# Last MoE of a two-layer trunk: expert rows added to x in SBUF by one-hot matmuls instead of scatter-adds to DRAM

## The chip, the cores and the metric

The kernel runs on 1 core of one Trainium2 chip. The metric is the device time of one execution in microseconds (us), the median of the runs shown. The profile and the trace come from one further execution on the same core; line numbers (L1236) are those of the kernel before.

## What is computed

A trunk of two layers. Each layer has a mixer and then an expert-choice mixture of experts (MoE): every expert takes the 64 latent tokens (of 512) with the highest routing weight, and its output rows are added to x. In the first layer a stream of 256 context tokens goes through the same experts; the second, last layer has the 512 latent tokens only, and its x is the output.

```python
def _expert_choice_ffn(h, router_w, w_gate, w_up, w_down):
    b, n_tok, _ = h.shape
    cap = EC_CAPACITY * n_tok // N_EXPERTS            # 2 * 512 // 16 = 64
    probs = jax.nn.softmax((h @ router_w).astype(jnp.float32), axis=-1)
    aff, idx = lax.top_k(jnp.swapaxes(probs, 1, 2), cap)
    xs = h[bidx, idx]
    hid = jax.nn.silu(einsum('becd,edf->becf', xs, w_gate)) * einsum('becd,edf->becf', xs, w_up)
    out = jnp.einsum('becf,efd->becd', hid, w_down) * aff[..., None]
    return jnp.zeros_like(h).at[bidx, idx].add(out.astype(h.dtype))
...
xl = xl + g2_l * _expert_choice_ffn(_modulate(_rms(xl, norm2_g[i]), sh2_l, sc2_l), ...)
```

All is float32. D_MODEL and MOE_FF are 1024, there are 16 experts, and the weights of one expert are three matrices of 1024x1024, 12.6 MB.

## The kernel before

The work of the last layer's MoE runs in two functions. `outer` (L1123) finishes the mixer's output projection, so that x stands in SBUF as the tile `xl` (128 x 4 x 1024, in pool `big`); routes it (`route_`, which leaves in `st` the token numbers `g` for gathers, the routing weights `af`, and the row numbers `sc`); writes the normalized rows to DRAM (`xh_l`, L1076); starts the gather of the first two experts' rows (`moe_gather`, L1189); and writes x itself to the output in DRAM (`base_write`, L1184), on which the experts then add. `experts` (L1246) loops over the 16 experts e = 0 to 15:

- `load_experts` issues the six loads of an expert on SP's queue: two halves each of `wg`, `wu`, `wd`, 2 MB a load, in the order of use. The buffers are taken in a ring written out by hand, `WT1 = "mmbbbbnnnb"`: ten buffers from three pools, so load n waits for TensorE (PE) to be done with load n - 10. The last letter is the fifth buffer of `big`, the one in which x stood.
- `gate_up` (L1236): for each half j (gate, up), 8 blocks k and 2 halves h a matmul of the 64 gathered rows against 512 columns; in the trace such a float32 matmul is two MATMUL rows, 64 rows for an expert. Then silu on ScalarE (ACT, L1239) and the product on VectorE (DVE, L1240) give `hid`.
- `turn_hid` (L1305, L1306): four transposes of `hid` on PE into `hT`, copied back by ACT.
- `down` (L1321, L1324): 32 MATMUL rows against `wd` into `oe`; partitions 0 to 63 hold the first 512 columns of the 64 rows, 64 to 127 the second 512. DVE scales by the routing weight and the gate into `ob`, and GpSimd (POOL, L1325) issues an indirect DMA that adds the 128 half rows of `ob` to rows `sc` of the output in DRAM (a scatter-add).
- After an odd e the rows of the next two experts are gathered (L1189) and transposed (`moe_turn`, L1198, L1203, L1205).

The tiles `hT` and `oe` share four PSUM buffers of the pool `b`; `gu` and `gT` share two of the pool `d`. In the last layer the order of the instructions on an engine is set by the framework's scheduler, and each engine carries it out in that order.

## Time and profile before

| | |
|---|---|
| median of 3 runs | 2016.27 us (2015.25 to 2017.24) |
| the profiled execution | 2015.42 us |
| its span, first to last instruction | 2013.7 us |
| PE busy in the span | 1824.0 us (91%) |
| DVE, ACT, POOL busy | 823.0, 586.4, 119.2 us |
| bytes moved by DMA | 545.62 MB, 271 GB/s over the span |

The span is 1.72 us shorter than the time of the same execution. The stages follow one another: the first layer's mixer to about 480 us, its experts to about 1090, the second mixer to about 1530, and the last layer's experts from there to the end. A profile row of the timeline gives start, length, engine, line, operation, output<-input, count, and in brackets how long the engine had been idle before and what released it.

### The profile page before, as it was taken

The page shows a single profiled execution, that of the slowest core. Times are in us where ns is not written, and L with a number is a line of the kernel's source. Part 1 is how long each engine was busy: PE and PEld are TensorE (multiplying, and loading weights), DVE is VectorE, ACT ScalarE, POOL GpSimd, SP SyncE. Part 2 cuts the span into 40 slices and gives each one's busy share as a digit, 9 for nine tenths or more (in the row PEclk, how much of TensorE's full clock was granted, in tenths as well). Part 3 has the DMA queues.
Part 4 walks back from the last instruction along what each step waited for, and adds up shares of the span by engine and source line. Part 5 has one row for each costly group of instructions (what it writes and reads, how often), then busy time and mean ns, then how long its engine had stood idle before and what let it go on. Part 6 is the DMA issues. An engine that isn't in the chain of part 4 may idle for free.

```text
span 2013.7 us, 28802 instructions
## 1 busy us (share of the span) xinstructions
PE 1824.0 (91%) x11900; PEld 1058.1 (53%) x11900; DVE 823.0 (41%) x2016; ACT 586.4 (29%) x1240; POOL 119.2 (6%) x118
## 2 busy tenths in 40 slices
PE   6999999999799999999996989999985997878776
PEld 5788888677433333333333778986762422222222
DVE  5797876676610101011104597976752100000000
ACT  5656465424210101011103565554330000000000
POOL 0000000000010111011000000000000000000000
PEclk9999999999699999999997989999987999999999
DMA  8352433246499999999985543211448999999997
GB/s 311 131 188 83 160 113 112 83 161 254 165 373 403 404 402 404 411 403 402 397 348 191 176 149 104 73 33 58 177 192 355 417 417 417 423 417 416 424 418 275
DMA packets 76403, 545.62 MB, mean 271 GB/s; under 512 B 8720, under 2 KB 15008, under 8 KB 51952
## 3 DMA queue, kind: packets, MB, share of 16 engines
q1 hardware_dynamic: 61312, 501.26, 62.6%
q0 software_dynamic: 14960, 42.53, 7.1%
q8 instruction: 93, 1.52, 0.3%
q14 instruction: 38, 0.31, 0.0%
HBM read 522.25 MB, written 21.50 MB: 270 GB/s over the span
## 4 chain that ended last, share of the span: by engine, by line
PE 36%; issue 29%; DMA 21%; DVE 7%; ACT 3%; POOL 3%; POOLq 0%; SPq 0%; ACTq 0%; DVEq 0%
DMA w<-wu 6%; DMA w<-wg 6%; DMA w<-wd 4%; PE gu L1236 4%; PE pt L416 3%; PE pt L418 2%; PE pt L417 2%; PE ao L839 2%; PE pf L416 2%; PE pf L417 2%; PE pf L418 2%; DMA xh_l<-xo 2%; PE ro L727 2%; PE macc L276 2%; PE oe L1321 1%
## 5 line engine op out<-in xcount | busy, mean ns | idle before, releaser
L1236 PE MATMUL gu<-w,xsT 128*64 128x512 f32 x2048 | 476.4, 617 | 50.6 <-DMA w<-wu 32.8
L1236 PEld LDWEIGHTS gu<-w,xsT 128*64 128x64 f32 x2048 | 153.4, 142 | 350.9 <-issue 271.0
L1321 PE MATMUL oe<-w,hid 128*64 128x512 f32 x1024 | 234.6, 610 | 9.7 <-ACT hid L1306 9.6
L1240 DVE TENSOR_TENSOR hid<-hid,gu 128x512 f32<-128x512 f32 x32 | 22.0, 687 | 462.9 <-ACT hid L1239 462.9
L1239 ACT ACTIVATE hid<-gu 128x512 f32<-128x512 f32 x32 | 19.1, 597 | 526.0 <-PE gu L1236 526.0
L1321 PEld LDWEIGHTS oe<-w,hid 128*64 128x64 f32 x1024 | 74.3, 140 | 157.1 <-issue 138.6
L417 PE MATMUL pt<-ws,hh 128*128 128x256 f32 x448 | 127.9, 285 | 5.0 <-DVE ws L411 5.0
L416 PE MATMUL pt<-ws,hh 128*128 128x256 f32 x448 | 130.8, 292 | 0.0
L418 PE MATMUL pt<-ws,hl 128*128 128x256 f32 x448 | 128.1, 286 | 0.0
L1324 DVE SCALAR_TENSOR_TENSOR ob<-oe,afl,g 128x512 f32<-128x512 f32 x32 | 24.0, 751 | 221.4 <-PE oe L1321 221.4
L1293 PE MATMUL guc<-w,xsT 128*32 128x512 f32 x1024 | 113.2, 594 | 0.0
L410 ACT ACTIVATE ws<-wraw 128x256 fp32r<-128x256 f32 x192 | 72.8, 411 | 83.6 <-PE pt L418 31.9
L416 PEld LDWEIGHTS pt<-ws,hh 128*128 128x128 f32 x448 | 85.8, 191 | 9.1 <-issue 8.6
L411 DVE TENSOR_TENSOR ws<-wraw,ws 128x256 fp32r<-128x256 f32 x192 | 76.7, 419 | 33.6 <-ACT ws L410 33.2
L417 PEld LDWEIGHTS pt<-ws,hh 128*128 128x128 f32 x448 | 85.7, 191 | 5.7 <-DVE ws L411 5.5
L418 PEld LDWEIGHTS pt<-ws,hl 128*128 128x128 f32 x448 | 85.8, 191 | 0.1
L1205 ACT ACTIVATE xsT<-gT,ab 128x128 f32<-128x128 f32 x80 | 36.6, 458 | 144.2 <-PE gT L1198 116.8
L416 PE MATMUL op<-ws,mh 128*128 128x256 f32 x256 | 74.9, 293 | 3.1 <-ACT mh L908 3.1
L817 ACT ACTIVATE p<-sc,mx 128x768 f32<-128x768 f32 (+1 forms) x80 | 65.2, 816 | 33.9 <-DVE mx L815 30.5
L417 PE MATMUL op<-ws,mh 128*128 128x256 f32 x256 | 74.0, 290 | 0.0
L418 PE MATMUL op<-ws,ml 128*128 128x256 f32 x256 | 73.5, 289 | 0.3 <-DVE ml L909 0.3
L815 DVE TENSOR_REDUCE mx<-sc 128x1 f32<-128x768 f32 (+1 forms) x80 | 66.4, 847 | 10.8 <-PE sc L811 10.2
(385 smaller groups left out, 3187.1 us busy)
## 6 DMA issues: line engine op xcount, KB each, us to landing
w<-wg SPq DMA_DIRECT2D x63, 2048.0 KB, 26.4
w<-wd SPq DMA_DIRECT2D x63, 2048.0 KB, 22.9
w<-wu SPq DMA_DIRECT2D x62, 2048.0 KB, 16.1
mw<-mod_w SPq DMA_DIRECT2D x80, 512.0 KB, 4.3
wraw<-w_in SPq DMA_DIRECT2D x48, 512.0 KB, 3.6
wo<-wo SPq DMA_DIRECT2D x24, 384.0 KB, 3.5
mw<-mod_a SPq DMA_DIRECT2D x16, 512.0 KB, 10.7
xh_l<-xo POOLq DMA_DIRECT2D x8, 512.0 KB, 12.4
```

The source lines that it names most:

```text
L276: nc.tensor.matmul(acc[32 * q:32 * q + 32, :256], self.scT[:, k, :], wt[:, q * 256:(q + 1) * 256], start=k == k0, stop=k == k0 + 1)
L410: nc.scalar.activation(t[:, 0], src, AF.Copy)
L411: nc.vector.tensor_tensor(t[:, 1], src, t[:, 0].bitcast(F32), op=ALU.subtract)
L416: nc.tensor.matmul(out, lh, rh, start=first, stop=False)
L417: nc.tensor.matmul(out, lh, rl, start=False, stop=False)
L418: nc.tensor.matmul(out, ll, rh, start=False, stop=last)
L727: nc.tensor.matmul(ol[64 * h:64 * h + 64, :], v, ws[h][:, :L], start=t == 0, stop=t == 5)
L815: nc.vector.tensor_reduce(mx, s[:, :n], axis=AX.X, op=ALU.max, negate=True)
L817: nc.scalar.activation(ptl[m][:, :n], s[:, :n], AF.Exp, bias=mx, accum_out=sm[:, m, t:t + 1])
L1236: self.pe(nc.tensor.matmul(d[64 * h:64 * h + 64, j, :], xl[:, k, x0:x0 + CAPL], W(j, k)[:, h * 512:(h + 1) * 512], start=k == 0, stop=k == ...
L1293: self.pe(nc.tensor.matmul(dc[32 * q:32 * q + 32, :], xc[:, k, c0:c0 + CAPC], W(q // 2, k)[:, (q % 2) * 512:(q % 2) * 512 + 512], start=k ...
L1321: self.pe(nc.tensor.matmul(o[64 * h:64 * h + 64, :], hid[:, 1, c * P + hh * 64:c * P + hh * 64 + 64], W(2, k)[:, h * 512:(h + 1) * 512], s ...
```

## The change

The routine `base_write` is no longer called in the last layer, and `xl` stays in its buffer: the ring of weight buffers has nine places. After `down` the rows `ob` go to a new function `combine`. It makes two one-hot matrices of 128x512 (DVE compares the numbers 0, 2, 4, ... with the row numbers, for each half h), splits `ob` into a rounded part `hi` (ACT) and the rest `lo` (DVE), both in the format float32r, and, for each of the 4 token tiles and both halves, lets PE multiply the one-hot columns with `hi` and `lo` into a PSUM tile `cb`, which DVE adds to x in SBUF. After the last expert each token tile is written to the output on SP's queue. The first layer is unchanged.

```diff
-WT1 = "mmbbbbnnnb"
+WT1 = "mmbbbbnnn"
...
+        if i == DEPTH - 1:
+            r["sf"] = self.cst([NE], nm="sf")
+            nc.vector.tensor_copy(r["sf"], sc)
...
-            self.base_write(x, base, not ctx or s)
+            if ctx:
+                self.base_write(x, base, s)
...
+        if not ctx:
+            self.iota = self.t("iota", [L], "iota")
+            nc.sync.dma_start(self.iota, self.a["iota2"])
...
-            self.down(e, W, hid, st[0], bl)
+            ob = self.down(e, W, hid, st[0])
+            if ctx:
+                self.scatter(bl, ob, st[0], e)
+            elif e < NE - 2:
+                late = lambda e=e, ob=ob: self.combine(e, ob, st[0])
+            else:
+                late = None
+                self.combine(e, ob, st[0], base_l if e == NE - 1 else None)
...
+    def combine(self, e, ob, st, dst=None):
+        nc = self.nc
+        oh = []
+        for h in range(2):
+            t = self.t("oh", [L], "oh", F32R)
+            nc.vector.tensor_scalar(t, self.iota, st["sf"][:, e:e + 1], -float(h), op0=ALU.subtract, op1=ALU.is_equal)
+            oh.append(t)
+        hi = self.t("obs", [L], "obh", F32R)
+        lo = self.t("obs", [L], "obl", F32R)
+        nc.scalar.activation(hi, ob, AF.Copy)
+        nc.vector.tensor_tensor(lo, ob, hi.bitcast(F32), op=ALU.subtract)
+        for t in range(4):
+            for h in range(2):
+                p = self.b("cb")
+                nc.tensor.matmul(p, oh[h][:, t * P:(t + 1) * P], hi, start=True, stop=False)
+                nc.tensor.matmul(p, oh[h][:, t * P:(t + 1) * P], lo, start=False, stop=True)
+                xx = self.xt[0][:, t, h * 512:(h + 1) * 512]
+                nc.vector.tensor_tensor(xx, xx, p, op=ALU.add)
+            if dst is not None:
+                nc.sync.dma_start(dst[t * P:(t + 1) * P], self.xt[0][:, t])
...
-            k.open(cw, ob=(2 if not last else 6, 0), g2=(2 if not last else 1, 0))
+            k.open(cw, ob=(2, 0), g2=(2 if not last else 1, 0))
...
+                k.open(cw, iota=(1, 0), oh=(2, 0), obs=(2, 0))
```

The tile `cb` comes from the same four PSUM buffers as `hT` and `oe`.

Line numbers in listings of the changed program are those of the changed kernel. What the change does to the order on PE, between the `down` of one expert and that of the next, in the middle of the last layer. Before (`oe` is the product with wd, `gu` the gate and up products, one matmul of the listing being two MATMUL rows of the trace, `hT` the transposes):

```order
L1305 MATMUL hT_14119<-ident_66,hid_14114 128x128 x4
L1321 MATMUL oe_14143<-w_14077,hid_14114 64x512 x8
L1321 MATMUL oe_14143<-w_14079,hid_14114 64x512 x8
L1236 MATMUL gu_14175<-w_14163,xsT_14134 64x512 x8
L1236 MATMUL gu_14175<-w_14165,xsT_14134 64x512 x8
```

Now, at the same place (`obh`, `obl` are `hi` and `lo`):

```order
L1361 MATMUL oe_14257<-w_14153,hid_14188 64x512 x8
L1348 MATMUL cb_14332<-obh_14328,oh_14324 128x512
L1348 MATMUL cb_14336<-obh_14328,oh_14326 128x512
L1348 MATMUL cb_14340<-obh_14328,oh_14324 128x512
L1348 MATMUL cb_14344<-obh_14328,oh_14326 128x512
L1349 MATMUL cb_14332<-obl_14329,oh_14324 128x512
L1349 MATMUL cb_14336<-obl_14329,oh_14326 128x512
L1241 MATMUL gu_14288<-w_14276,xsT_14248 64x512 x8
L1349 MATMUL cb_14340<-obl_14329,oh_14324 128x512
L1349 MATMUL cb_14344<-obl_14329,oh_14326 128x512
L1348 MATMUL cb_14348<-obh_14328,oh_14324 128x512
```

The first product with `obh` stands directly behind the last product into `oe`, ahead of the next expert's `gu`; the other four pairs follow the first quarter of `gu`. From expert 3's rows on it is so for every expert. For the rows of experts 0, 1 and (for five of its eight pairs) 2 the pairs stand elsewhere on PE, at the end of the next expert's `gu` and ahead of its `hT`:

```order
L1241 MATMUL gu_13550<-w_13544,xsT_13510 64x512 x8
L1348 MATMUL cb_13594<-obh_13590,oh_13586 128x512
L1349 MATMUL cb_13594<-obl_13591,oh_13586 128x512
L1348 MATMUL cb_13598<-obh_13590,oh_13588 128x512
...
L1349 MATMUL cb_13622<-obl_13591,oh_13588 128x512
L1320 MATMUL hT_13626<-ident_66,hid_13583 128x128 x4
L1241 MATMUL gu_13663<-w_13651,xsT_13510 64x512
L1361 MATMUL oe_13632<-w_13546,hid_13583 64x512 x8
```

There a whole `gu` lies between `oe` and the pairs. At the end of the program DVE's order is now this, `ob` being the last thing there before:

```order
L1364 SCALAR_TENSOR_TENSOR ob_15244<-oe_15227,afl_13269,g_2195_13379 128x512
L1344 TENSOR_TENSOR obl_15251<-ob_15244,obh_15250 128x512
L1351 TENSOR_TENSOR xl_12287<-xl_12287,cb_15254 128x512
L1351 TENSOR_TENSOR xl_12287<-xl_12287,cb_15258 128x512
...
L1351 TENSOR_TENSOR xl_12287<-xl_12287,cb_15285 128x512
```

Eight additions of 128x512 now stand behind the last `ob`, and SP's four writes of x to the output behind those.

## Rows read from the trace of the kernel before

**Rows 1.** Page, 40 slices: tenths of a slice in which PE and DMA were busy.
```profile
PE   6999999999799999999996989999985997878776
...
DMA  8352433246499999999985543211448999999997
```
**Rows 2.** Stretches: length; busy us of PE, PEld, DVE, ACT, POOL; clock; DMA; GB/s.
```profile
1600.00:1996.00 396.00, 317.73 (x1356) 102.03 (x1358) 28.71 (x51) 27.11 (x51) 25.26 (x18) 0.94 1.01 418
...
2005.00:2009.00 4.00, 0.00 (x0) 0.00 (x0) 0.00 (x0) 0.00 (x0) 0.07 (x1) 0.83 0.50 66
```
**Rows 3.** The same columns, one expert each: with and without a gather.
```profile
1776.39:1808.25 31.86, 24.67 (x108) 8.27 (x108) 2.56 (x6) 2.43 (x5) 2.56 (x2) 0.95 1.01 419
1808.25:1838.95 30.70, 23.91 (x102) 7.23 (x100) 1.97 (x3) 1.79 (x3) 1.57 (x1) 0.94 1.01 418
```
**Rows 4.** The same columns: 10 us without and 10 us with a scatter-add's packets.
```profile
1685.00:1695.00 10.00, 8.76 (x42) 2.64 (x40) 0.75 (x1) 0.00 (x0) 1.57 (x1) 1.00 1.01 431
...
1695.00:1705.00 10.00, 6.30 (x28) 1.70 (x26) 0.00 (x0) 0.00 (x0) 0.00 (x0) 0.94 1.02 395
```
**Rows 5.** Timeline of PE, experts 2 to 9 of the last layer.
```profile
1601.57 8.72 PE L1321 MATMUL oe<-w,hid 128*64 128x512 f32 x32 [0.69 <-ACT hid L1306]
...
1628.32 8.79 PE L1321 MATMUL oe<-w,hid 128*64 128x512 f32 x32 [0.69 <-ACT hid L1306]
1636.93 13.90 PE L1236 MATMUL gu<-w,xsT 128*64 128x512 f32 x64
1652.32 0.66 PE L1305 MATMUL hT<-ident,hid 128*128 128x128 f32 x4 [1.48 <-DVE hid L1240]
1653.66 7.09 PE L1321 MATMUL oe<-w,hid 128*64 128x512 f32 x32 [0.69 <-ACT hid L1306]
...
1664.96 1.09 PE L1198 MATMUL gT<-ident,gath 128*128 128x128 f32 x8
...
1840.50 8.72 PE L1321 MATMUL oe<-w,hid 128*64 128x512 f32 x32 [0.69 <-ACT hid L1306]
```
**Rows 6.** Timeline of PE: the products with wd of expert 0 and of expert 15.
```profile
1554.98 7.17 PE L1321 MATMUL oe<-w,hid 128*64 128x512 f32 x32
...
1995.37 7.09 PE L1321 MATMUL oe<-w,hid 128*64 128x512 f32 x32 [0.69 <-ACT hid L1306]
```
**Rows 7.** Timeline of SP's queue: the load of the tenth buffer.
```profile
1539.00 0.33 SPq L1223 DMA_DIRECT2D w<-wu  x1
```
**Rows 8.** Nearest for a float32r product of 512 columns: PE in the first mixer.
```profile
29.42 0.39 PE L417 MATMUL pf<-hl,ws 128*128 128x512 f32 x1
29.65 0.40 PE L418 MATMUL pf<-hh,ws 128*128 128x512 f32 x1
```
**Rows 9.** Nearest for hi, lo (ns min/median/max) and the addition (busy us, mean ns).
```profile
L398 ACT ACTIVATE hh<-h x16: 616/624/633, 26.4 to 1108.7; 128x512 fp32r<-128x512 f32 x16
...
L399 DVE TENSOR_TENSOR hl<-h,hh x16: 681/684/693, 28.1 to 1109.3; 128x512 fp32r<-128x512 f32 x16
...
L1240 DVE TENSOR_TENSOR hid<-hid,gu 128x512 f32<-128x512 f32 x16 | 11.0, 687 | 242.6 <-ACT hid L1239 242.6
```
**Rows 10.** Timeline behind the last product: ob on DVE, the last scatter-add on POOL.
```profile
2002.50 0.75 DVE L1324 SCALAR_TENSOR_TENSOR ob<-oe,afl,g 128x512 f32<-128x512 f32 x1 [8.53 <-PE oe L1321]
2003.53 1.54 POOL L1325 DMA_INDIRECT out_dram<-ob,sl  x1 [29.09 <-DVE ob L1324]
```
**Rows 11.** The program's closing instructions: ns min/median/max, first and last start.
```profile
L1464 SPq EVENT_SEMAPHORE  x11: 17/28/28, 2008.3 to 2013.6; - x11
L1464 POOLq EVENT_SEMAPHORE  x4: 17/17/17, 2012.9 to 2013.5; - x4
```
**Rows 12.** DMA issues: KB each, median us from issue to landing.
```profile
out_dram<-xl POOLq DMA_DIRECT2D x4, 512.0 KB, 6.6
...
xr_c<-xc POOLq DMA_DIRECT2D x2, 512.0 KB, 4.0
```

More of the change, by code (lines that the diff above doesn't have):

```diff
@@ L1120, in route_ @@
             nc.vector.tensor_scalar(sc[o], tt[:, 1], float(nq), float(q), op0=ALU.mult, op1=ALU.add)
-        return {"g": g, "af": af, "sc": sc}
+        r = {"g": g, "af": af, "sc": sc}
+        if i == DEPTH - 1:
+            r["sf"] = self.cst([NE], nm="sf")
+            nc.vector.tensor_copy(r["sf"], sc)
+        return r
     def outer(self, i, m, xs, xsrc, g1, free, base_l, base_c):
@@ L1277, in experts @@
                 late = lambda e=e, W=W, hc=hc: self.down_c(e, W, hc, st[1], bc)
-        if late is not None:
+        if ctx:
             late()
@@ L1313, in turn_hid_c, with scatter, down @@
         nc.scalar.activation(hc[:, 512:], hT[:, :256], AF.Copy)
-    def down(self, e, W, hid, st, bl):
+    def scatter(self, dst, ob, st, e):
+        self.nc.gpsimd.indirect_dma_start(out=dst, out_offset=bass.IndirectOffsetOnAxis(ap=st["sc"][:, e:e + 1], axis=0),
+                                          in_=ob, in_offset=None, compute_op=ALU.add)
+    def combine(self, e, ob, st, dst=None):
[18 more added lines that the diff above has]
+                nc.sync.dma_start(dst[t * P:(t + 1) * P], self.xt[0][:, t])
+    def down(self, e, W, hid, st):
         nc = self.nc
@@ L1324, in down @@
         nc.vector.scalar_tensor_tensor(ob, o, st["af"][:, e:e + 1], self.g2[0], op0=ALU.mult, op1=ALU.mult)
-        nc.gpsimd.indirect_dma_start(out=bl, out_offset=bass.IndirectOffsetOnAxis(ap=st["sc"][:, e:e + 1], axis=0),
-                                     in_=ob, in_offset=None, compute_op=ALU.add)
+        return ob
     def down_c(self, e, W, hc, st, bc):
@@ L1339, in down_c @@
                                        op0=ALU.mult, op1=ALU.mult)
-        nc.gpsimd.indirect_dma_start(out=bc, out_offset=bass.IndirectOffsetOnAxis(ap=st["sc"][:, e:e + 1], axis=0),
-                                     in_=oc, in_offset=None, compute_op=ALU.add)
+        self.scatter(bc, oc, st, e)
 def emit(ctx, tc, a, out):
@@ L1371, in emit @@
                     st, xl = k.outer(i, ms[i], xs, src[1], g1, free, *base)
-            k.open(cw, ob=(2 if not last else 6, 0), g2=(2 if not last else 1, 0))
+            k.open(cw, ob=(2, 0), g2=(2 if not last else 1, 0))
             if not last:
                 k.open(cw, gathc=(1, 0), xsc=(2, 0), hidc=(2, 0), oc=(1, 0))
+            else:
+                k.open(cw, iota=(1, 0), oh=(2, 0), obs=(2, 0))
             k.open(cw, b=(4, 1), d=(2, 1))
@@ L1453, in layouts @@
     r["blk"] = blk
+    r["iota2"] = cc(np.broadcast_to(2 * np.arange(L, dtype=f), (P, L)))
     for nme, w in (("wg", exp_w_gate), ("wu", exp_w_up), ("wd", exp_w_down)):
```

## The prediction

> **What bounds the kernel now.** I read the slices first, then stretches, then PE's timeline, then the end. The change lies in the last layer's experts, the last quarter of the span. There DMA is busy throughout and PE is not [rows 1]: from 1600 to 1996 us the DMA share is 1.01 at 418 GB/s, while PE is busy for 317.73 of 396 us [rows 2]. An expert takes 30.70 us, or 31.86 when a gather falls into it [rows 3]. Its weights are 12.58 MB; at the 431 GB/s of a stretch without other traffic [rows 4] they need 29.2 us, so a gather costs some 1.2 us and a scatter-add some 1.5 us. The bytes of a scatter-add (0.262 MB) would need only 0.6 us at that rate; the stretch in which its packets move shows the loss, 395 GB/s with its own bytes counted in [rows 4]. So the weights' stream is the bound, and the change takes load off it.
>
> The second thing to see is how close PE is behind. Expert 4 ran without a wait for weights [rows 5]: 13.90 us of gate and up, 1.48 us of waiting for the product `hid`, 0.66 of transposes, 0.69 of waiting for the copy, 7.09 of down. That is **23.82 us**, against a stream that without scatter-adds would need 29.2 or 30.4. PE has about 6 us to spare for an expert, and the change gives it new work.
>
> The third is the end. The last down ends at 1995.37 + 7.09 = 2002.46 [rows 6], and the span ends 11.24 us later: `ob`, the scatter-add [rows 10], then closing instructions. The last packets move within 2005 to 2009 [rows 2], SP starts closing at 2008.3, and POOL only at 2012.9 [rows 11].
>
> **The change part by part.**
>
> *Off the DMA queues.* Fifteen scatter-adds in the stream at 1.5 us (at least 0.6 by bytes) are 22 us of DMA time (at least 9). The write of x (2.1 MB) goes too, but it stood ahead of the stream, where no expert load could yet be issued: I cost it at nothing; the cover is that PE starts expert 0 from loads long landed. The iota load (0.26 MB) costs 0.6 us there, also covered.
>
> *One weight buffer less.* The load of the tenth buffer was issued at 1539.00, when x was written out [rows 7]; now it waits for the first half of `wg` to be used, about 1540. It is the second half of expert 1's `wu`, which PE wants at 1562.15 + 10 = 1572. Thirty us are ample for a load of 2.1 MB / 431 GB/s = 4.87 us and its fixed time, so I cost it at nothing. Later, each buffer comes free one load earlier in the ring, and the stream keeps two or three loads queued. From 1540 the remaining 87 loads and six gathers need 87 x 4.87 + 6 x 1.2 = 431 us: the stream could end at 1971, 25 us sooner than the 1996 of before.
>
> *New on PE.* 16 products an expert. The nearest rows are float32r products of 512 columns, which start 0.23 us apart [rows 8]; with 0.235 this is **3.76 us**. Below lies 15 x 0.21, the pace of the 64 MATMUL rows in 13.90 us [rows 5]; above, every product at its full 0.40 us, 6.4. I take the pace since four products with `hi` stand in a row.
>
> *A new wait on PE.* From expert 3's rows on, the first one-hot product stands directly behind down in PE's order, and it needs `ob` and then `hi`. While PE waits there, the next expert's whole gate and up is queued behind it, though its weights have landed. The wait is 0.04 of handing over (2002.46 to 2002.50), 0.75 for `ob` [rows 10], 0.04, 0.62 for `hi` on ACT [rows 9], 0.04: **1.49 us**. `lo` takes 0.68 on DVE [rows 9], less than the four products with `hi` (0.94), so nothing more is waited for there. DVE's eight additions at 0.69 [rows 9] take 5.8 us and lie under gate and up; the last pairs have their PSUM buffers by then, within 0.1 us.
>
> So an expert costs PE 23.82 + 1.49 + 3.76 = **29.07 us**, and 1.1 more for the transposes of a gather [rows 5]. That is what the stream needs, but PE does not have the stream's start: when PE begins, nine loads of 96 are done. PE becomes the bound.
>
> *Experts 1 to 3.* Here the pairs stand between up and `hT`, where PE waits 1.48 us anyway. Only four PSUM buffers are there, so the last pairs go at the pace of the additions, and so does `hT`, whose buffer is freed by one. Bounds are 23.82 + 3.76 - 1.48 = 26.1 and 29.07; I take 26.3, near the lower, as the first four pairs need no addition. Three make 79 us.
>
> *The sum for PE at full clock.* Expert 0's down ends at 1554.98 + 7.17 = 1562.15 as before [rows 6]; + 79 = 1641; twelve experts at 29.07 and five gathers at 1.1 make 354; the last down ends at **1995.3**, 7 us sooner than before.
>
> *PE's clock.* The down of experts 2 and 3 took 8.72 and 8.79 us instead of 7.09 [rows 5]: the granted clock fell to 1.2 GHz after the waits of 1.48 and 0.69 us around `hT`, at 1.68 us a time. Four of the fifteen downs behind such waits are that long (first and last in [rows 5]); of the three where PE had run unbroken up to the wait, experts 2 to 4, two are. After the change PE runs unbroken, keeps these waits in twelve experts, and gets the 1.49 us one. I take a fall in half of them, 6 x 1.68 = **10.1 us**, between 3 and 8 of 12 by the two shares; bounds are none and all twelve, 0 and 20 us. Last down: 2005.4, 3.0 later than before. The Trainium skill, page TensorE: Matmul & The Clock Gate, section "A second HAM failure mode: psum-queue depth-cycling", speaks against this change: it reports a kernel that cycled through PSUM banks and, by small idle gaps between groups of products, kept swinging between both clock levels. By that rule the fall comes with every expert, and the sum would have 20 us here; this trace shows it in only some.
>
> *The end.* `ob` and `hi` 1.49, four products 0.94, the first `lo` product 0.4, then eight additions at 0.69 + 0.03 that wait for nothing else, 5.8: 8.6 us. The last of four writes of x (0.5 MB) is issued then; the nearest rows land in 4.0 us, or 6.6 with others beside it [rows 12]; three lie before it, each 1.3 us at 431 GB/s and 1.4 us apart, so 4.0. POOL's last work is then a gather far earlier, so its late closing should go, and what stays is the 0.8 us from 2012.9 to the end [rows 11] and SP's 0.5. Together 13.9 us (12 to 18), against 11.24: **+2.7**.
>
> **Sum:** 3.0 + 2.7 = +5.7 us on the profiled execution's 2015.42, which is 0.85 under the median. On the median this is 2016.27 + 5.7 = **2022**. About 0.2% (4 us) is what a measurement here can tell from no change.
>
> **Rivals.**
> - *The clock stays up* in nearly all experts (0 to 3 falls). For it: expert 4 shows the same waits and no fall. Against it: experts 2 and 3 [rows 5]. The time: 2022 - 10.1 = 2012 with none, 2017 with three.
> - *The clock falls in every expert*, on the slower side: each wait around `hT` behind an unbroken gate and up brings a down at 8.7. It decides from 6 falls on, where slower begins. 12 x 1.68 = 20.2 instead of 10.1: 2032. For it speak experts 2 and 3, against it expert 4. It is what the rule of the Trainium skill on PSUM cycling would do here, and so far the trace bears that out in part.
> - *DMA stays the bound and its saving is the gain.* It needs PE under some 28 us an expert, so that the products hide in PE's waits for weights. The stream ends at 1971 instead of 1996, and the last down 6.5 us behind it: 25 - 2.7 = 22 us gained, 1994. Against it: 29.07 without a single fall.
> - *The lost buffer starves PE.* If a load comes late by one slot, PE waits 4.87 us: 2027. Against it is the 30 us of lead; it would need DMA at under 418 GB/s.
> - *The change does nothing*, as its new wait and its saving cancel: that is the middle of the forecast's own spread, not a mechanism of its own.
>
> **Numbers.** The forecast (4 to 8 falls, 2018 to 2025) has 0.55; clock up 0.18; falls everywhere 0.14; lost buffer 0.07; DMA bound 0.06. Faster by over 0.2%, under 2012.2, are DMA bound and the part of clock up with no or one fall at slightly lower terms: 0.17. Slower, over 2020.3: falls everywhere, lost buffer, and somewhat over half of the forecast: 0.53. Within: 0.30. The range takes in clock up and falls everywhere, 2011 to 2032, and leaves out DMA bound and the outer edges; the forecast's own range is 2015 to 2028.
>
> **What would show it.** Right: in the new timeline PE has a wait of about 1.5 us on `hi` behind down in experts 3 to 14, starts of one-hot products 0.23 us apart, an expert near 29 us at full clock, hardly any wait for `wg` or `wu`, some downs at 8.7 us; DMA share under 0.97 and the last weights landed 15 us or more before the last down; some 14 us behind it. Wrong: waits for weights still there after expert 5 (then DMA bounds), an expert much under 28 us of PE, products 0.4 us apart, or a closing of POOL that still ends 9 us after the last product.

## The result, and the profile after

| | before | the changed kernel |
|---|---|---|
| median of 6 runs | 2016.12 us (2010.27 to 2017.75) | 2026.3 us (2022.34 to 2029.26) |
| ratio to before, 95% interval | | 1.0054 (1.0037 to 1.0071) |
| the profiled execution, and its span | 2015.42, 2013.7 us | 2028.67, 2026.9 us |
| bytes moved by DMA | 545.62 MB | 541.72 MB |
| written to DRAM | 21.50 MB | 17.30 MB |

The change makes the kernel slower by half a per cent, 10.2 us by the medians; 5.7 us was forecast, a time of 2022. The page's slices show the exchange of roles: PE is busier in the last quarter, at 8 tenths where 7 and 8 stood, and DMA is as busy as before [rows 1].

```profile
PE   6999999998799999999996989999976998888887
...
DMA  8352433247499999999985533112447999999992
```

In stretches (length; busy time of PE, PEld, DVE, ACT, POOL; granted clock; DMA share; GB/s): the first row is the middle of the last layer's experts [rows 2], the next two are one expert each, without and with a gather [rows 3], the last is the end of PE's work.

```profile
1600.00:1975.00 375.00, 334.42 (x1495) 134.57 (x1491) 110.64 (x191) 33.70 (x62) 4.70 (x5) 0.99 1.01 427
1648.62:1678.27 29.65, 25.97 (x116) 9.82 (x116) 7.89 (x14) 1.82 (x3) 0.00 (x0) 1.00 1.01 428
1678.27:1709.10 30.83, 27.15 (x124) 10.64 (x124) 9.52 (x18) 3.66 (x7) 0.94 (x1) 1.00 1.01 427
...
1985.00:2014.56 29.56, 26.77 (x116) 10.16 (x116) 7.05 (x12) 1.82 (x3) 0.00 (x0) 1.00 0.01 4
```

The reader is to see two things. The stream runs at 427 GB/s as long as it lasts, and then PE works on for 30 us with no transfer beside it: the weights are there, and PE is late. And PE waits for no weights. In the kernel before, PE stood idle ahead of gate and up products until these loads had landed (us, times), 48.6 us in all:

```profile
  DMA w<-wu: 32.8, 16
  DMA w<-wg: 15.8, 14
```

In the changed kernel's groups of the last layer (busy us, mean ns, then idle time and what ended it) they wait for none; what PE waits for is the first product with `hi`, 1.58 us in each of 13 experts, and `hT`:

```profile
L1241 PE MATMUL gu<-w,xsT 128*64 128x512 f32 x1024 | 233.2, 600 | 0.7 <-ACT xsT L1210 0.6
L1361 PE MATMUL oe<-w,hid 128*64 128x512 f32 x512 | 118.9, 616 | 8.5 <-ACT hid L1321 8.5
L1348 PE MATMUL cb<-obh,oh 128*128 128x512 f32 x128 | 47.2, 418 | 20.7 <-ACT obh L1343 20.5
L1349 PE MATMUL cb<-obl,oh 128*128 128x512 f32 x128 | 46.9, 402 | 0.0
L1320 PE MATMUL hT<-ident,hid 128*128 128x128 f32 x64 | 10.4, 285 | 18.5 <-DVE hid L1245 18.5
```

PE's timeline through one expert at full clock, and into a down at the lower one [rows 5]:

```profile
1760.94 7.09 PE L1361 MATMUL oe<-w,hid 128*64 128x512 f32 x32 [0.69 <-ACT hid L1321]
1769.60 1.19 PE L1348 MATMUL cb<-obh,oh 128*128 128x512 f32 x4 [1.57 <-ACT obh L1343]
1770.62 0.61 PE L1349 MATMUL cb<-obl,oh 128*128 128x512 f32 x2
1771.17 3.65 PE L1241 MATMUL gu<-w,xsT 128*64 128x512 f32 x16
1774.75 0.73 PE L1349 MATMUL cb<-obl,oh 128*128 128x512 f32 x2
...
1777.29 10.52 PE L1241 MATMUL gu<-w,xsT 128*64 128x512 f32 x48
1789.23 0.66 PE L1320 MATMUL hT<-ident,hid 128*128 128x128 f32 x4 [1.42 <-DVE hid L1245]
1790.57 8.78 PE L1361 MATMUL oe<-w,hid 128*64 128x512 f32 x32 [0.69 <-ACT hid L1321]
```

The scheduler cut the gate and up products into a quarter and three quarters, with six one-hot products ahead of the first and ten ahead of the rest. From down to the first product PE waits 1.57 us, as forecast (1.49).

The end, by the timeline [rows 6, 10], the closing instructions [rows 11] and the DMA issues [rows 12]:

```profile
2007.47 7.09 PE L1361 MATMUL oe<-w,hid 128*64 128x512 f32 x32 [0.69 <-ACT hid L1321]
...
2014.61 0.75 DVE L1364 SCALAR_TENSOR_TENSOR ob<-oe,afl,g 128x512 f32<-128x512 f32 x1 [8.53 <-PE oe L1361]
2015.46 0.63 ACT L1343 ACTIVATE obh<-ob 128x512 fp32r<-128x512 f32 x1 [8.04 <-DVE ob L1364]
...
2017.60 4.87 DVE L1351 TENSOR_TENSOR xl<-xl,cb 128x512 f32<-128x512 f32 x8 [0.79 <-PE cb L1349]
...
2018.92 3.92 SPq L1353 DMA_DIRECT2D out_dram<-xl  x4
```
```profile
L1505 SPq EVENT_SEMAPHORE  x11: 17/28/28, 2022.9 to 2026.8; - x11
L1505 POOLq EVENT_SEMAPHORE  x4: 17/17/17, 2025.8 to 2026.8; - x4
```
```profile
out_dram<-xl SPq DMA_DIRECT2D x4, 512.0 KB, 2.8
```

From the last down's end, 2014.56, to the end of the span are 12.3 us (11.24 before). POOL's closing row now stands 2.9 us behind SP's first one, about the 2.8 us in which the last write of x lands; before, it stood 4.6 us behind.

**Where the 13.2 us between the two spans lie.** The first product of the last MoE starts at 1541.22 instead of 1536.53, 4.7 us later, with nothing changed ahead of the last router. From there to the end of the last down it takes 473.3 us instead of 465.9, +7.4. Behind it +1.1.

### The profile page after: what moved, and what is told of

Its sections match the earlier page's. It is cut to its first block, busy times and chain, and to the rows that moved or that the text cites. A ratio compares the mean times of both kernels' runs of the same rounds, so it can differ in the third digit from the quotient of the medians.

```text
span 2026.9 us, 29447 instructions
## 1 busy us (share of the span) xinstructions
PE 1874.3 (92%) x12156; PEld 1111.2 (55%) x12156; DVE 926.2 (46%) x2193; ACT 597.1 (29%) x1256; POOL 91.6 (5%) x98
## 2 busy tenths in 40 slices
DMA packets 74246, 541.72 MB, mean 267 GB/s; under 512 B 8481, under 2 KB 14769, under 8 KB 49793
## 3 DMA queue, kind: packets, MB, share of 16 engines
HBM read 522.51 MB, written 17.30 MB: 266 GB/s over the span
## 5 line engine op out<-in xcount | busy, mean ns | idle before, releaser
L1241 PE MATMUL gu<-w,xsT 128*64 128x512 f32 x2048 | 459.8, 599 | 1.7 <-ACT xo L1075 1.0
L1351 DVE TENSOR_TENSOR xl<-xl,cb 128x512 f32<-128x512 f32 x128 | 79.3, 682 | 78.8 <-PE cb L1349 78.8
```

Source lines behind the costliest of these rows:

```text
L1241: self.pe(nc.tensor.matmul(d[64 * h:64 * h + 64, j, :], xl[:, k, x0:x0 + CAPL], W(j, k)[:, h * 512:(h + 1) * 512], start=k == 0, stop=k == ...
L1351: nc.vector.tensor_tensor(xx, xx, p, op=ALU.add)
```

## The experiments

The theory was that PE is the bound after the change, because of where the one-hot products stand; the rivals were the stream, the ninth buffer, the number of products, and the clock. Each ratio is to runs of the kernel before that were taken beside the same experiment; their medians were 2014.1 us (experiments 1 to 4), 2014.3 (5 to 8), 2012.5 (9 and 10) and 2014.5 (11 and 12). In the short diffs, - is the changed kernel (or the kernel before, where that is said). "Falls" are stretches between the first product of the last MoE and its last down in which the granted clock is at its lower level, 1.2 GHz, counted in stretches of 1 us, without the low clock in which all fourteen kernels start that stage; each of them took 1.65 to 1.71 us of full clock, but for two of experiment 7, which are twice as long. Where an expectation speaks of a second kernel of 2002 us, it is experiment 2; "the other kernel" in the expectation of experiment 4 is experiment 1.

| kernel | median us | ratio to before (95%) | first product | falls |
|---|---|---|---|---|
| before (profile) | 2015.42 | | 1536.53 | 14 |
| changed (profile 2028.67) | 2026.3 | 1.0054 (1.0037 to 1.0071) | 1541.22 | 3 |
| 1 products behind gate and up | 2003.75 | 0.9951 (0.9933 to 0.9968) | 1539.11 | 0 |
| 2 and in the last but one | 2001.96 | 0.9940 (0.9924 to 0.9957) | 1538.13 | 0 |
| 3 `hi` only | 2012.21 | 0.9994 (0.9984 to 1.0004) | 1539.54 | 10 |
| 4 products right behind down | 2037.41 | 1.0117 (1.0101 to 1.0134) | 1537.03 | 8 |
| 5 before, nine buffers | 2012.55 | 0.9997 (0.9987 to 1.0007) | 1535.73 | 8 |
| 6 before, no scatter-adds | 1988.3 | 0.9869 (0.9855 to 0.9884) | 1536.71 | 5 |
| 7 as 2, `hi` only | 2000.73 | 0.9932 (0.9918 to 0.9947) | 1539.65 | 6, two of them double |
| 8 as 2, products behind `hT` | 2002.72 | 0.9944 (0.9929 to 0.9958) | 1538.78 | 0 |
| 9 before, one more input | 2014.45 | 1.0007 (0.9998 to 1.0016) | 1535.94 | 9 |
| 10 before, one more constant | 2017.61 | 1.0019 (1.0009 to 1.0029) | 1539.66 | 11 |
| 11 as 2, constant moved | 2001.52 | 0.9934 (0.9920 to 0.9948) | 1536.52 | 0 |
| 12 changed, constant moved | 2022.39 | 1.0037 (1.0023 to 1.0050) | 1533.13 | 4 |

### 1. The products behind the next expert's gate and up

```diff
-        self.fixed = ctx
+        self.fixed = True
...
-                nc.tensor.matmul(p, oh[h][:, t * P:(t + 1) * P], hi, start=True, stop=False)
+                self.pe(nc.tensor.matmul(p, oh[h][:, t * P:(t + 1) * P], hi, start=True, stop=False))
```
(and the same for `lo`)

> PE in the last MoE is held to program order, so the 16 products of an expert stand behind the gate and up products of the next one in all experts, not only in 1 to 3. Theory (after is bound by PE, which stands 1.57 us behind each down for the two parts of the rows and 1.42 us for the activation, and products of 0.235 us): an expert costs 26.6 us of PE as in experts 1 to 3 of after (79.86 / 3), less than a stream of weights needs (29.2, and 1.2 for a gather in every second expert), so PE catches up with the stream, idle time for weights comes back (tens of us), the last weights land at about 1972 to 1977, the last down ends at 1977 to 1985 and the span at 1990 to 1998: 1991 to 2000 us, below both kernels. Rival A (the stream or the ninth buffer holds the kernel, whatever PE's order): no change, 2022 to 2029. Rival B (PE, which waits for weights again, gets the lower clock in every expert): the slow downs (8.75 us against 7.1) come back and 2003 to 2010 is what is left.

Measured: 2003.75 us, below before and 22.5 us below the changed kernel. PE's timeline in an early expert, and in expert 14:

```profile
1637.18 7.09 PE L1361 MATMUL oe<-w,hid 128*64 128x512 f32 x32
1644.10 13.90 PE L1241 MATMUL gu<-w,xsT 128*64 128x512 f32 x64
1657.93 0.50 PE L1348 MATMUL cb<-obh,oh 128*128 128x512 f32 x1
1658.27 0.39 PE L1349 MATMUL cb<-obl,oh 128*128 128x512 f32 x1
...
1662.43 0.65 PE L1320 MATMUL hT<-ident,hid 128*128 128x128 f32 x4
1663.77 0.65 PE L1361 MATMUL oe<-w,hid 128*64 128x512 f32 x2 [0.69 <-ACT hid L1321]
...
1939.21 3.65 PE L1241 MATMUL gu<-w,xsT 128*64 128x512 f32 x16 [0.96 <-DMA w<-wu]
1944.11 3.65 PE L1241 MATMUL gu<-w,xsT 128*64 128x512 f32 x16 [1.25 <-DMA w<-wu]
```

From down to down are 26.59 us (1663.77 - 1637.18; the last of these rows is cut by the window), without the wait for `hi` and without the wait ahead of `hT`, which the products now cover. So the place of the products cost 29.65 - 26.6 = 3 us an expert, and the theory of the place holds. PE catches up with the stream in expert 8 and from there waits for weights again:

```profile
L1241 PE MATMUL gu<-w,xsT 128*64 128x512 f32 x854 | 189.4, 594 | 19.5 <-DMA w<-wu 16.7 <-DMA w<-wg 2.7
```

The forecast of the time, 1991 to 2000, was missed by 4 us. I had the stream end at 1972 to 1977; its last bytes move at about 1981.5 (the rate is 124 GB/s from 1980 to 1985). PE's last wait for weights is the one at 1944.11 above; behind it come the rest of expert 14, the whole of expert 15 and the new end, 58.5 us up to 2002.6. Rival A falls; of rival B nothing is seen, no fall in the experts.

### 2. The same in the last but one expert

```diff
-            elif e < NE - 2:
+            elif e < NE - 1:
```
(on top of experiment 1)

> As the kernel with PE in program order, and the products of the last but one expert too stand behind the gate and up products of the last one. Theory (the end of the stream sets the end): the products of that expert, 4 us, move under the wait for the last down weights; 1.5 us of waiting and up to 4 us of products come off where PE is still behind the stream at that point, nothing where it already waits for weights: 0 to 5 us below the kernel without this edit. Rival (PE still sets the end): 1.5 us only. Second rival: the products now delay the last turn and the last down, 0 to 4 us slower.

Measured: 2001.96, 1.8 us below experiment 1, within the theory's 0 to 5; the two intervals overlap, so the step is not resolved by time. The timeline shows what the edit was for: PE now arrives early enough to wait for the last `wu`.

```profile
1967.97 7.09 PE L1241 MATMUL gu<-w,xsT 128*64 128x512 f32 x32 [1.27 <-DMA w<-wu]
...
1980.83 7.09 PE L1361 MATMUL oe<-w,hid 128*64 128x512 f32 x32 [0.69 <-ACT hid L1321]
```

From this wait to the end of the span, 2000.1, are 32 us of PE work and closing. That is what the stream's end does not hide.

### 3. Half the products, in the changed kernel's order

```diff
-        lo = self.t("obs", [L], "obl", F32R)
-        nc.vector.tensor_tensor(lo, ob, hi.bitcast(F32), op=ALU.subtract)
...
-                nc.tensor.matmul(p, oh[h][:, t * P:(t + 1) * P], hi, start=True, stop=False)
-                nc.tensor.matmul(p, oh[h][:, t * P:(t + 1) * P], lo, start=False, stop=True)
+                nc.tensor.matmul(p, oh[h][:, t * P:(t + 1) * P], hi, start=True, stop=True)
```

> Leaves out the products with the rest part (and the subtraction that makes it), so the rows are added only to the precision of the first part; 8 products an expert instead of 16, in after's own order. Theory (PE bound, 0.235 us a product): an expert costs 8 x 0.235 = 1.9 us less and some 0.1 us less for waiting on the rest part; 16 experts: 30 us less, 1.9 of it behind the last down, so 1994 to 1999, or somewhat more where PE catches up with the stream (29.8 us an expert) before the end. Rival A (the stream or the ninth buffer binds): 0 to 3 us. Rival B (what costs is a fixed price of waiting and switching for each expert, not the number of products): 10 us or less.

Measured: 2012.21, 14 us less, not 27 to 32: a miss by half. The timeline of an expert, from its first one-hot product (1709.92) to the next expert's:

```profile
1709.92 1.78 PE L1346 MATMUL cb<-obh,oh 128*128 128x512 f32 x5 [1.57 <-ACT obh L1342]
1711.64 3.65 PE L1241 MATMUL gu<-w,xsT 128*64 128x512 f32 x16
...
1738.40 1.78 PE L1346 MATMUL cb<-obh,oh 128*128 128x512 f32 x5 [1.85 <-ACT obh L1342]
```

It takes 28.48 us, but the wait at its end is 0.28 longer than the one at its start; from the end of one down to that of the next (1708.35 to 1736.55) it is 28.20 us instead of 29.65: 1.45 us saved, not 1.9. Five products take 1.72 us, 0.34 each and not 0.235, since each needs a PSUM buffer of its own and there are four, freed by additions of 0.61 us. And the waits are all still there, as large or larger (1.57 and 1.85 here). From the first product of the stage to the end of its last down it is 466.7 us instead of 473.3, 6.6 less, with 10 falls against 3; seven falls at 1.7 us are 12, so at full clock some 18.5 us are saved, and 0.9 more behind the last down. Of the forecast 30 us, then, a third was never there, and part of the rest went to the clock. This profile, of 2019.44 us, is the slowest of ten runs, whose others lie between 2010.99 and 2016.38. Their mean granted clock over the whole program is 0.964 to 0.967, and 0.962 here; by the medians of the runs the loss to the low clock is some 5 us larger than in the changed kernel (estimated from these shares of the span, in which falls of earlier stages count too), and 19 - 5 = 14 is what the medians differ by.

### 4. The products right behind each down, in all experts

```diff
-        self.fixed = ctx
+        self.fixed = True
...
-                late = lambda e=e, ob=ob: self.combine(e, ob, st[0])
+                self.combine(e, ob, st[0])
```
(products held to program order, as in experiment 1)

> PE in program order, with the products of every expert right behind its own down, experts 0 to 2 too; the reverse of the order that the other kernel of this call tries. Theory (the place of the products costs 29.65 - 26.6 = 3.0 us an expert without gather): three more experts at 3.0 us, 9 us above after, 2033 to 2038; some of it less where PE starts an expert without the split of the gate and up products in quarters that after has. Rival A (PE's order makes no difference): 2022 to 2029. Rival B (holding PE to program order is itself what helps or harms): it differs from after by as much as the other order does.

Measured: 2037.41, as the theory has it, 33.7 us above experiment 1 with the same instructions and the same way of ordering them. So it is the place, not the fixing. Some 14 of the 33.7 us are its eight falls of the clock, of which experiment 1 has none. The trace also shows that a fall of the clock need not hit a down. Stretches of 2 us (columns as above):

```profile
1716.00:1718.00 2.00, 1.52 (x4) 1.04 (x5) 1.11 (x2) 0.19 (x1) 0.00 (x0) 0.81 0.96 408
1718.00:1720.00 2.00, 2.00 (x6) 1.51 (x6) 1.65 (x3) 0.00 (x0) 0.00 (x0) 0.50 1.06 453
1720.00:1722.00 2.00, 2.00 (x9) 1.51 (x7) 1.77 (x3) 0.00 (x0) 0.00 (x0) 0.83 1.00 426
```

The clock is at 0.50, 1.2 GHz, behind the wait for `hi`, and the one-hot products start 0.43 us apart there instead of 0.23. No down of this profile is long, and yet it has eight falls.

### 5 and 6. The lost buffer and the scatter-adds, each by itself

```diff
-WT1 = "mmbbbbnnnb"
+WT1 = "mmbbbbnnn"
```
(experiment 5, on the kernel before)

> The kernel before with nine weight buffers instead of ten in the last layer; nothing else. Theory as revised by the traces of the first four runs (a tenth load filled a gap in the stream: in the kernel before it is issued at 1539.0, with nine buffers the next load waits for the first half of wg to be used, 1544 to 1547, and the DMA moves only 56 to 115 GB/s for 10 to 15 us): 5 to 8 us of the stream lost, all of it in the end because the stream binds before: 3 to 7 us slower than before. Theory as predicted (the lost buffer costs nothing): within 2 us of before. Rival (nine buffers starve PE later too, expert by expert): 10 us or more slower.

Measured: 2012.55, ratio 0.9997 (0.9987 to 1.0007). My revised theory falls and the prediction stands: the buffer costs nothing here. SP's queue fits this. With nine buffers the first load that needs a used buffer goes out at 1540.52, 1.5 us later than the tenth buffer's load before [rows 7], because x had to be written out of that buffer first.

```profile
1540.52 0.33 SPq L1223 DMA_DIRECT2D w<-wu  x1
```

In the changed kernel it goes out at 1546.99, 6.5 us later than here: its first products start 5.5 us later (1541.22 instead of 1535.73), and the rest is the lower clock, which lasts until 1545. So with nine buffers the stream goes on only when PE has begun. Whether that costs anything without scatter-adds can be read from experiments 6 and 11, which start at 1536.71 with ten buffers and at 1536.52 with nine: the third last load lands at 1980.15 and at 1979.65. The lost buffer and the write of x that goes cost the stream nothing together; each by itself is not shown there.

```diff
+        if self.fixed:
             nc.gpsimd.indirect_dma_start(out=bl, out_offset=...
```
(experiment 6, on the kernel before: `self.fixed` is true in the first layer alone)

> The kernel before without the 16 scatter-adds of the last MoE (it leaves the experts' rows out of the output). What the removed part is worth by itself where the stream binds. Theory from the first runs (an expert that waits for weights takes 29.5 and 30.9 us by turns without scatter-add, 30.70 and 31.86 with it: 1.1 us each): 15 x 1.1 = 17 us, and the end behind the last down shrinks from 11.2 us to 3 to 5: 22 to 26 us less, 1988 to 1993. Theory as predicted (1.5 us of DMA for each): 22 and 7 us, 29 less, 1983 to 1987. Rival (the scatter-adds were hidden): under 10 us less.

Measured: 1988.3, 26.0 us less. The last down:

```profile
1977.81 7.09 PE L1321 MATMUL oe<-w,hid 128*64 128x512 f32 x32 [0.90 <-DMA w<-wd]
```

It ends at 1984.90 instead of 2002.46 [rows 6]: 17.6 us for fifteen scatter-adds in the stream, **1.17 us each**. By the landing of the last load, 1982.65 instead of 1998.78, it is 16.1 us, 1.08 each; the other 1.4 us lie in PE's last expert, in which the clock falls once in the kernel before and not here. The span ends 1.8 us behind it instead of 11.24, so 9.4 us of the end were the last scatter-add and what closes behind it: 27.0 us by the spans. This is the whole price of the scatter-adds; the write of x, which the change removes too, is still there.

### 7 and 8. Is PE's time free once the stream binds?

Experiment 7 is experiment 2 with the edit of experiment 3, experiment 8 is experiment 2 with the products one place later:

```diff
-            if late is not None:
+            if late is not None and ctx:
                 late()
             self.turn_hid(hid)
+            if late is not None and not ctx:
+                late()
```

> Leaves out the products with the rest part, in the order that stands behind the gate and up products in all experts; against the second kernel of the first call (2002 us) it has 8 products an expert less. Theory (with that order the stream sets the time until the last half of wu has landed, about 1968): only the products behind that point count, those of the last two experts, and they are paced by the additions on VectorE (0.61 us each): 1 to 4 us less, 1998 to 2001. Rival (products cost their 1.9 us an expert in any order): 20 to 30 us less.

> As the second kernel of the first call (2002 us), but the products stand one place later: behind the turn of the activation (hT) and ahead of the down, so that the 1.42 us wait for the activation stays and the 0.69 us wait behind the turn is covered. Theory (the stream binds, PE has about 3 us an expert to spare): PE's expert is 0.7 us longer, which the waits for weights take up; only the last expert shows it: 0 to 2 us slower than 2002. Rival A (PE's own time counts in every expert): 11 us slower. Rival B (the waits of PE bring the slow clock back): each fall costs 1.7 us; up to 16 of them, where PE is not waiting for weights anyway.

Measured: 2000.73 and 2002.72, against 2001.96. Both as the theory has it. Eight products fewer an expert are worth 1.2 us in all, which the intervals do not tell from nothing, though 14 us in the other order. (The profile of experiment 7 has six stretches at the lower clock where that of experiment 2 has none, and no loss by them shows in the time.) And a PE that takes 27.1 us instead of 26.7 for each of experts 1 to 7 (downs from 1556.78 to 1746.50, against 1556.39 to 1743.02) loses under 1 us. With the products behind gate and up, an expert has some 3 us of PE to spare.

### 9 to 12. The start of the last MoE

What was still open was the later start, in all seven traces of kernels with the change, of work that the change does not touch. The candidates were the added input in DRAM and the added constant tile.

```diff
+    r["iota2"] = cc(np.broadcast_to(2 * np.arange(L, dtype=f), (P, L)))
```
(experiment 9, on the kernel before; the input is not read)

> The kernel before with one more input in DRAM (the row of even numbers that the changed kernel loads, 256 KB), declared at the same place among the inputs and never read. In three profiles of kernels without it the last MoE's first product starts at 1535.7 to 1536.7 us; in seven with it at 1537.0 to 1541.2, and the writes of xh_l land in 13.1 to 13.6 us (median) instead of 12.0 to 12.5, though nothing before that point was changed. Theory (the new input moves the other tensors in DRAM, and the writes in the first layer's router land later): xh_l 13.1 to 13.6 us, first product of the last MoE at 1538 to 1541, 1 to 4 us slower than before. Rival (scatter of the runs, or another part of the change): 12.0 to 12.5 us, 1536, same time as before.

```diff
+            r["sf"] = self.cst([NE], nm="sf")
+            nc.vector.tensor_copy(r["sf"], sc)
```
(experiment 10, on the kernel before, last layer only; the tile is not read)

> The kernel before with the float copy of the last layer's row numbers that the changed kernel makes (one 16-column constant tile, which moves what is allocated behind it on the chip by 64 bytes a partition, and one VectorE copy of it in the last router), never read. Theory of the added input in DRAM: no change, xh_l 12.0 to 12.5 us, first product of the last MoE at 1536, same time as before. Rival (the later start comes from the constant tile or its copy): xh_l 13.1 to 13.6 us, first product at 1538 to 1541, 1 to 4 us slower.

Measured: experiment 9 starts at 1535.94 and its time is that of before within the interval; experiment 10 starts at 1539.66 and is 0.19% (0.09 to 0.29) slower. The theory of the input falls, with its sign too: the writes of `xh_l` land in 10.4 and 10.2 us here, neither 12 nor 13 (and in 13.0 and 13.3 in experiments 11 and 12, which start early). So the tile was taken out of the constants:

```diff
-            r["sf"] = self.cst([NE], nm="sf")
-            nc.vector.tensor_copy(r["sf"], sc)
...
+            st[0]["sf"] = self.t("sf", [NE], "sf")
+            nc.vector.tensor_copy(st[0]["sf"], st[0]["sc"])
```
(from the router to `experts`, in a pool opened there; 11 on experiment 2, 12 on the changed kernel)

> The second kernel of the first call (2002 us, ratio to before 0.9940), with the float copy of the row numbers in a small tile that is opened for the experts of the last MoE instead of among the constants, so that nothing ahead of that point is moved on the chip. Theory (the constant tile makes the kernel start the last MoE later: first product at 1539.7 with the tile alone and at 1537.0 to 1541.2 in seven kernels of the change, at 1535.7 to 1536.7 in four kernels without it): first product at 1535.5 to 1537, 2 to 4 us less, 1998 to 2000. Rival (scatter of the runs, or the rest of the change): first product at 1537 to 1541, 2001 to 2004.

> The changed kernel itself with the same move of the float copy out of the constants, and nothing else. Theory of the constant tile: first product of the last MoE at 1535.5 to 1537 instead of 1541.2, 2 to 4 us less: 2022 to 2024, which is where the prediction's sum stood. Rival: no change, 2025 to 2028. Falls of the clock in the last MoE (3 in the changed kernel's profile, 1.7 us each) may be more or fewer by chance, 2 us either way.

Measured: the first products start at 1536.52 and 1533.13. All eight profiles with the tile among the constants start between 1537.0 and 1541.2, all six without it between 1533.1 and 1536.7; the means are 1539.1 and 1535.8. That the edit shifts the start by some 3 us is shown by this grouping. It isn't VectorE's copy that does it, which takes 0.18 us at 1524.8 in experiment 10: by then the shift is there. On average over the same two groups the first layer's router products start at 488.1 us with the tile among the constants and at 486.4 without, and the first layer's last down, of the context rows, ends at 1078.6 and 1075.7. What is left of the edit is that the tile lies among the constants and moves what lies behind it; how that makes the stages slower is not shown. What the shift is worth at the end stays unresolved: the changed kernel's median goes from 2026.3 to 2022.39, though the two intervals overlap (1.0037 to 1.0071 and 1.0023 to 1.0050), and experiment 11 is only 0.4 us below experiment 2. The two profiles of the changed kernel and of experiment 12 differ mainly by the start: from the first product to the end of the span they take 485.7 and 486.4 us.

Experiment 11 keeps the whole computation and is, with experiment 2, the fastest such version: ratio 0.9934 (0.9920 to 0.9948), 13 us below before and 25 below the change as it was made.

## Why the prediction was right, and where it was off

The time, 2026.3, lies in the range (2011 to 2032) and on the forecast's side. Point by point:

- **The bound passes from the stream to PE**: right. No wait for weights is left in the experts. But "DMA share under 0.97" is wrong, it is 1.01 at 427 GB/s: both are near their limits, 30 us apart in time. The stream brings loads from 1547 to about 1984 (the share of 1975 to 1990 is 0.62), PE works from 1541 to 2014.6.
- **The wait for `ob` and `hi`**, 1.49 us: 1.57. **Sixteen products**, 3.76 us: 4.11. **An expert at full clock**, 29.07: 29.65. This term was mis-sized by 0.58, and most of the missing part lies where PE changes from one kind of product to the other: the gate and up products, unbroken 13.90 us [rows 5], take 14.10 in two pieces (1771.17 to 1774.75, then 10.52), and the one-hot products take 1.57 us for six (1.41 at the pace) and 2.54 for ten (2.35). In experiment 1 too the first one-hot product behind gate and up is followed by the next after 0.34 us (1657.93 to 1658.27) and not 0.23. I had priced the products at the pace of a row of their own kind and nothing for the change from float32 products (128*64 in the rows) to float32r ones (128*128) and back; which of these differences costs it, no run separates. Over twelve experts it is 7 us.
- **Experts 1 to 3**, 79 us: 79.9 (from the end of one down, 1567.19, to that of the third next, 1647.05). This was the step that mattered most: it says that the products cost 2.8 us less in that place, and it was used only as a detail of three experts.
- **Falls of the clock**: six of twelve were forecast, 10.1 us; the profile has three, 5.1 us. The size of each was right (1.70, forecast 1.68), the share was not. The Trainium skill, page TensorE: Matmul & The Clock Gate, section "A second HAM failure mode: psum-queue depth-cycling", reports a kernel whose cycling through PSUM banks kept the clock swinging; as the prediction applied it, a fall would come with every expert. The traces have 3 falls in the changed kernel, 8 to 10 in experiments 3 and 4, and none in experiments 1, 2 and 8, which cycle through the same four PSUM buffers, so the rule is borne out in part only.
- So the two errors in the experts, +7 and -5, nearly cancel: with +0.9 for experts 1 to 3, +0.4 for gathers at 1.18 instead of 1.1, and +0.35 for expert 0, the forecast +3.0 becomes +6.7, and +7.4 was measured. The rest is the last expert, which takes 30.44 us (1984.12 to 2014.56) and not 29.65: there the one-hot products stand in two groups of eight with two rows of gate products between. (The prediction's own terms add up to 1995.5; it wrote 1995.3.) That the experts came out so near the forecast is luck as much as sizing.
- **The end**, +2.7: +1.1. The additions took 0.61 us each when they follow one another (4.87 for eight), not 0.72, and the last write of x landed in 2.8 us, not 4.0. That POOL's late closing goes was right.
- **The start**: "Expert 0's down ends at 1554.98 + 7.17 = 1562.15 as before" is the step that failed outright. It ends at 1567.19, and experiments 10 to 12 put some 3 us of that on the constant tile, which the prediction did not look at: it asked where each new instruction stands in time, but not what a new tile moves. The rest of the 5 us is within what the starts scatter by in either group, and 0.35 of expert 0's own.
- **The stream's end at 1971 and 22 us for fifteen scatter-adds**: the price was 1.1 to 1.2 us each, not 1.5, so 16 to 18 in all. In the changed kernel the stream ends near 1984; it starts late (1546.99 instead of 1540) and its rate is 427 and not 431 GB/s. None of this shows in the changed kernel's time, for there PE sets the end; in experiment 1 the stream ends 4 to 9 us behind the end that was expected.
- **The lost buffer costs nothing**: right in the kernel before (experiment 5); without scatter-adds shown only together with the write of x (experiments 6 and 11).
- **The write of x costs nothing**: not tried by itself.
- Of the rivals, "DMA stays the bound and its saving is the gain" was right in its condition, "PE under some 28 us an expert": with the order of experiment 1 that condition holds. The saving it gave was too large: the time is 2002 to 2004, where 1994 was given.

The mechanism is then this. The change saves the stream 1.1 to 1.2 us an expert and 9.4 us at the end, 26 us in all by the medians (experiment 6), and it gives PE 16 products an expert. Where they stand in the changed kernel, 3 us of waiting an expert come with them (1.57 for `hi`, and the 1.42 ahead of `hT` that they no longer cover), PE needs more time than the stream, and the whole saving and 10 us more are lost. Where they stand behind the next expert's gate and up, they fill a wait that PE has anyway, PE keeps ahead, and half of the saving remains. The other half is 13.4 us by the spans of experiments 2 and 6: 10.4 for the new end (12.1 us behind the last down instead of 1.8) and 3.0 for a last down that ends later (1987.92 and 1984.90).

## What to carry to other kernels

When work moves from a DMA queue to an engine, its place in that engine's order is worth more than its amount: the same sixteen products cost 29.65 or 26.6 us an expert, by whether the engine waits for their input or fills an old wait with them, and once the place was right, leaving half of them out gained nothing that the runs resolve. The scheduler stood the first one-hot product directly behind its producer here; look at the listing for a first consumer on the engine that is about to become the bound, and hold it back by one stage. And price a new kind of product with its neighbours, since each change between kinds cost 0.1 to 0.2 us here, and look at what a new constant tile moves, not only at what it computes.

## What the hardware showed unexpectedly

- A fall of TensorE's clock in this stage takes 1.65 to 1.71 us of full clock, some 3.4 us at 1.2 GHz (two of experiment 7 are double), and it hits whatever runs behind the wait: downs (8.78 us instead of 7.09), one-hot products (0.43 us apart instead of 0.23), or, in the kernel before, gate and up products behind a wait for weights. Counting long downs, as the prediction did, misses these; the timeline of before has 14 falls and four downs over 8.7 us.

```profile
1672.12 5.35 PE L1236 MATMUL gu<-w,xsT 128*64 128x512 f32 x16 [2.30 <-DMA w<-wu]
1678.29 3.65 PE L1236 MATMUL gu<-w,xsT 128*64 128x512 f32 x16 [0.82 <-DMA w<-wu]
```

- What decides that it falls stays open. The same waits of 1.57, 1.42 and 0.69 us around a down gave 3 falls in the changed kernel, 8 in experiment 4 and 10 in experiment 3, and experiment 1, which waits 20 us for weights in pieces of about 1 us and 0.69 us in each expert, has none.
- A scatter-add of 0.26 MB takes 1.1 to 1.2 us of the stream, about twice the 0.6 us of its bytes at 431 GB/s, and as the last transfer of the program it held the end for 9.4 us (experiment 6).
- A constant tile of 64 bytes a partition that nothing reads made a kernel 0.19% (0.09 to 0.29) slower (experiment 10); the last stage starts some 3 us later on average in the profiles with it, and the delay grows from the first layer on.
